# Three one-bank score tiles and three transposed groups in the second attention, where scores have up to 512 columns

## The chip, the core and the metric

The kernel runs on one core of a Trainium2 chip. The metric is the device time of one execution in microseconds: the median of three runs before the change is 2951.13 us (2950.57 to 2956.34). A profiled execution, taken by the hardware profiler, gives the trace that is read below.

The core's engines work side by side, each on its own queue of instructions in a fixed order: TensorE (PE; its weight loads are listed apart as PEld), VectorE (DVE), ScalarE (ACT), GpSimd (POOL) and SyncE (SP), which issues the transfers. TensorE writes its results into PSUM, which this kernel uses as eight banks of 128 x 512 numbers of 4 bytes.

## The reference

One block of a transformer, 1024 positions, width 1024, float32: a gated feed-forward layer, a token mixer, a second feed-forward layer, each after an RMS norm and added to the stream. The mixer has two attentions. The first is a differential attention: 8 heads, each the difference of two softmaxes. The second (`nsa`) has 16 heads in 2 groups and three branches whose outputs are added with gates. One branch works on compressed keys and is done earlier in the kernel. The other two are what the change touches:

```python
s = jnp.where(mask[:, :, :, None], s, NEG_INF)          # selected blocks: at 1024 positions and
p = jax.nn.softmax(s.reshape(sh[:4] + (-1,)), axis=-1)  # 16 blocks of 64, all earlier keys
...
mask = (kpos[None, :] >= 0) & (kpos[None, :] <= qpos[:, None]) & (kpos[None, :] > qpos[:, None] - WIN)
p = jax.nn.softmax(s, axis=-1)                          # window of 512 keys
...
o = g[..., 0:1] * o_cmp + g[..., 1:2] * o_slc + g[..., 2:3] * o_win
```

Since 16 blocks are selected out of 16, the selected branch is causal attention over all earlier keys.

## The kernel before

The kernel runs its stages in this order: first feed-forward layer; the projections of the mixer with the compressed branch (`prelim`); the first attention (`da_phase`); the second (`ns_phase`); the output projections (`proj`); the second feed-forward layer. In the trace the second attention's scores and products lie between about 1478 and 2110 us.

In `ns_phase` the outer loops run over the two groups, then over pairs of heads `pr`, then over the two halves `H` of the positions, then over the two heads `par` of the pair, then over two blocks `m` of 256 queries. For one head and one `m`:

- `ns_scores` takes the two blocks of 128 queries `i = 2m` and `2m+1`. For each it makes two score tiles with `scores`: one of the selected branch, `w = 128 (i+1)` columns, 128 to 1024; one of the window branch, `ww`, at most 640. So in the half `H = 0` (`i` from 0 to 3) no tile has more than 512 columns, and in `H = 1` (`i` from 4 to 7) every tile has at least 640. One pair of heads and one `H` make 16 tiles.
- `scores` writes a tile `S` in PSUM with two matmuls for each piece of columns (L871; over 512 columns in two pieces, one a bank). VectorE adds the mask and takes the row minimum of the negated scores in one instruction (L878, with a short second one that reads the accumulator out). ScalarE takes the exponential into a tile of probabilities in SBUF, `Ps` or `Pw`, and sums the row (L880, again with a short second instruction). Then `S` is free. VectorE inverts the sums (L1034, L1035) and GpSimd scales the probabilities (L1037).
- `ns_pv` multiplies the probabilities by the values. `tr_split` transposes up to four 128 x 128 blocks into a bank `tr` (L926), ScalarE copies it to `th` and VectorE makes the rest `tl` (L89 and L85), each in SBUF; then the matmuls with the values add into the output bank `o` (L1083 with `th`, L1084 with `tl`). The compressed branch opens `o` (L1049), and `ns_fold` empties it (L1092, L1093).

The scores of a block are written in the program ahead of the products of the block before it (`pend`), so that TensorE has products to do while the other engines work on scores. A filler (`fill`) lays gemms of other stages between them at a lower priority and an even pace; these use the bank `gm` (L52 to L54).

The order of the instructions on each engine is not written by hand. A planner runs the program on a model of the engines, takes at each moment the instruction of the highest priority (mostly: the earliest in the program) that the model holds ready, and fixes that order. On the chip each engine then follows it, and waits where what it needs isn't there.

Buffers come from pools. A pool has a number of buffers, and a new tile waits until the last user of its buffer is done. All pools are opened with `reuse_waits="tile"`: a tile in a pool that lies where a closed pool lay waits for the last users of its own bytes (in PSUM, of its own bank) and for nothing else. In both attentions the banks are: two score tiles of two banks each (`sp`), two transposed groups (`tr`), one output bank (`ops`), one for the filler (`gm`). A score tile takes two banks whatever its width. The probabilities have five buffers of each kind (`B_NP`), the `th` and `tl` three (`B_NT`).

Of the kernel before, what the change touches and what calls it, by code (L numbers as in the profile page):

```python
# [7 lines left out]
F32 = mybir.dt.float32  # L8
# [10 lines left out]
P = 128  # L19
T = 1024  # L20
TB = 512
# [840 lines left out]
        nc.sync.dma_start(out=K.s_pc[u * 2 + pr][tb], in_=pp.bitcast(F32))  # L862


def scores(K, passes, w, mask, nm, pt, l):
    nc = K.nc
    S = K.sp.tile([P, T], F32, tag="S", name="S")
    pieces = [(0, 0, w)] if w <= TB else [(0, 0, w // 2), (TB, w // 2, w // 2)]
    for o, c, n in pieces:
        for i, (q, k, k0) in enumerate(passes):  # L870
            K.last = nc.tensor.matmul(S[:, o:o + n], lhsT=q, rhs=k[:, k0 + c:k0 + c + n], start=i == 0, stop=i == 1)  # L871
    if w <= TB:
        sv, mv, pv = S[:, 0:w], mask, pt[:, 0:w]
    else:
        sv = S.rearrange("p (b c) -> p b c", b=2)[:, :, 0:w // 2]
        mv = mask.rearrange("p (b c) -> p b c", b=2)
        pv = pt[:, 0:w].rearrange("p (b c) -> p b c", b=2)
    nc.vector.tensor_tensor_reduce(out=sv, in0=sv, in1=mv, scale=-0.125, scalar=BIG, op0=ALU.add, op1=ALU.min,  # L878
                                   accum_out=nm)
    return nc.scalar.activation(out=pv, in_=sv, func=AF.Exp, scale=-1.0, bias=nm, accum_out=l)  # L880
# [97 lines left out]
def da_load(K, h):  # L978
    drain([da_load_parts(K, h)])
# [317 lines left out]
B_NPC = 2  # L1297
LOW_DA = 20
LOW_NS = 100
TR_DA = 2  # L1300
PACE_DA = 16
PACE_NS = 140

# [1 line left out]
def da_phase(K, cg):  # L1305
    nc = K.nc
    with ExitStack() as ctx:
        K.kp, K.vp, K.qp = open_pool(K, ctx, "dk", B_DK), open_pool(K, ctx, "dv", B_DV), open_pool(K, ctx, "dq", B_DQ)
        K.nk, K.vv = {}, {}
        for n, f in enumerate(da_units(K, 0)[:2] + da_units(K, 1)):  # L1310
            if n == 2:
                early = da_load_parts(K, 0)
            if n >= 2:
                next(early)
            if n == 5:
                q0 = da_queries(K, 0, 0)
            drain([f()])
        cg.close()
        K.low = LOW_DA
        log_exp(K)  # L1320
        K.pp, K.sm, K.tp, K.op = (open_pool(K, ctx, "dp", B_DP), open_pool(K, ctx, "dsm", 6), open_pool(K, ctx, "dt", B_DT),
                                  open_pool(K, ctx, "do", 1))
        K.sp = open_pool(K, ctx, "sp1", 2, True)
        K.tr = open_pool(K, ctx, "tr1", TR_DA, True)
        K.ops = open_pool(K, ctx, "o1", 1, True)
        K.gm = open_pool(K, ctx, "gm1", 3 - TR_DA, True)
        pend = K.fin = None

        def finish(h, m, res):
            if m % 2 == 0:  # L1330
                K.o = K.ops.tile([P, TB], F32, tag="o", name="o")
            if K.fin:
                da_finish2(K, *K.fin)
                K.fin = None
            da_pv(K, h, m, res, K.o)
            if m % 2 == 1:
                K.fin = da_finish(K, h, m // 2, K.o)

        ng = NG_DA // 2
        W = K.A["win"]  # L1340
        units = []
        for p in (2, 3):
            cs = [[C_QDA + 2 * p, C_QDA + 2 * p + 1], [C_KDA + 2 * p, C_KDA + 2 * p + 1], [C_VDA + 2 * p], [C_VDA + 2 * p + 1]]
            units += [(f, [W[c] for c in ws]) for f, ws in zip(da_units(K, p), cs)]
        units += [(f, [W[C_GATE + c]]) for c, f in enumerate(gate_units(K, range(16)))]
        units += [(lambda d=d: pda_unit(K, d), [K.A["wda"][d]]) for d in range(KD)]
        fill = K.filler = Filler(K, units)
        for p in range(4):
            fill.pace(4 * (p + 1) if p < 2 else 8 + ng * (p - 1), PACE_DA)
            for h in (2 * p, 2 * p + 1):  # L1350
                if h:
                    da_load(K, h)
                for m in range(4):
                    qt = q0 if h + m == 0 else da_queries(K, h, m)
                    if h == 4:
                        ns_load_key(K, m)
                    res = da_scores(K, h, m, qt, fill.step)
                    if pend:
                        finish(*pend)
                    pend = (h, m, res)  # L1360
            fill.end()
        finish(*pend)
        da_finish2(K, *K.fin)


def ns_phase(K):
    nc = K.nc
    K.low = LOW_NS
    with ExitStack() as ctx:
# [2 lines left out]
        K.qp, K.kp, K.pcp = open_pool(K, ctx, "nq", 2), open_pool(K, ctx, "nk", 1), open_pool(K, ctx, "npc", B_NPC)  # L1372
        K.pp, K.sm, K.tp, K.op = (open_pool(K, ctx, "np", B_NP), open_pool(K, ctx, "nsm", 6), open_pool(K, ctx, "nt", B_NT),
                                  open_pool(K, ctx, "no", B_NO))
        K.sp = open_pool(K, ctx, "sp2", 2, True)
        K.tr = open_pool(K, ctx, "tr2", 2, True)
        K.ops = open_pool(K, ctx, "o2", 1, True)
        K.gm = open_pool(K, ctx, "gm2", 1, True)
        fill = K.filler
        fill.pace(8 + 16 + KD, PACE_NS)  # L1380
        ns_load_values(K)
# [30 lines left out]
        fill.end()  # L1412
        if pend:
            finish(*pend)


def proj(K, open_x, after):
# [54 lines left out]
def body(tc, A, out):  # L1472
    nc = tc.nc
    K = Ctx()
    K.tc, K.nc, K.A = tc, nc, A
    K.low, K.vv, K.gate, K.fill, K.seen = 0, {}, None, None, {}
    K.h, K.acc, K.R = [None] * 2, [None] * 2, [None] * 2
    with ExitStack() as ctx:
        const = open_pool(K, ctx, "const", 1)
# [172 lines left out]
```

## Time and profile before

| | |
|---|---|
| median of the runs | 2951.13 us (2950.57 to 2956.34) |
| profiled execution | 2957.75 us, span of its instructions 2955.7 us |
| TensorE busy, share of the span | 2830.8 us, 96% |
| TensorE weight loads | 2129.2 us, 72% |
| VectorE | 2002.1 us, 68% |
| ScalarE | 1366.1 us, 46% |
| GpSimd | 788.7 us, 27% |
| mean granted TensorE clock | 0.986 |

How to read it: times are microseconds unless marked ns. A group of instructions is named by its line in the kernel, its engine and what it writes and reads; behind its busy time stands the engine's idle time just before its instructions, and what ended it. A matmul's end is modelled and matmuls overlap in the array, so a busy TensorE can still have slack. A view of stretches gives, for each part of the time, its length and each engine's busy time in it.

### The profile page before, as it was taken

The page shows a single profiled execution, that of the slowest core. Times are in us where ns is not written, and L with a number is a line of the kernel's source. Part 1 is how long each engine was busy: PE and PEld are TensorE (multiplying, and loading weights), DVE is VectorE, ACT ScalarE, POOL GpSimd, SP SyncE. Part 2 cuts the span into 40 slices and gives each one's busy share as a digit, 9 for nine tenths or more (in the row PEclk, how much of TensorE's full clock was granted, in tenths as well). Part 3 has the DMA queues.
Part 4 walks back from the last instruction along what each step waited for, and adds up shares of the span by engine and source line. Part 5 has one row for each costly group of instructions (what it writes and reads, how often), then busy time and mean ns, then how long its engine had stood idle before and what let it go on. Part 6 is the DMA issues. An engine that isn't in the chain of part 4 may idle for free. (4 is left out here: it accounts for less than half of the span.)

```text
span 2955.7 us, 40158 instructions
## 1 busy us (share of the span) xinstructions
PE 2830.8 (96%) x14276; PEld 2129.2 (72%) x14276; DVE 2002.1 (68%) x3347; ACT 1366.1 (46%) x2347; POOL 788.7 (27%) x701
## 2 busy tenths in 40 slices
PE   8999999999999899989899999999999999999998
PEld 6644447888888678778788888888778854444886
DVE  7866856666687467667677777776343877675666
ACT  7543424442332245445466666666332653342443
POOL 3133321000144123322233323332242413333001
PEclk9999999999999999999999999999999999999999
DMA  4355548655456544444332234222742246454854
GB/s 161 129 194 180 182 161 287 214 172 170 146 200 240 173 161 168 170 165 164 122 115 79 86 119 155 79 84 76 281 158 100 89 147 230 149 185 158 297 182 146
DMA packets 212711, 478.20 MB, mean 162 GB/s; under 512 B 20896, under 2 KB 39584, under 8 KB 212512
## 3 DMA queue, kind: packets, MB, share of 16 engines
q1 hardware_dynamic: 212512, 475.65, 47.1%
q8 instruction: 112, 1.84, 0.3%
q14 instruction: 87, 0.71, 0.1%
HBM read 313.56 MB, written 162.00 MB: 161 GB/s over the span
## 5 line engine op out<-in xcount | busy, mean ns | idle before, releaser
L405 PEld LDWEIGHTS <-w 128*128 128x128 f16 x3024 | 297.1, 99 | 381.1 <-issue 30.4
L52 PE MATMUL gm<-hi,whi 128*128 128x512 f32 x880 | 351.5, 399 | 4.0 <-ACT whi L89 1.6
L54 PE MATMUL gm<-hi,wlo 128*128 128x512 f32 x880 | 348.3, 397 | 1.1 <-DVE wlo L85 1.1
L53 PE MATMUL gm<-lo,whi 128*128 128x512 f32 x880 | 348.0, 395 | 0.0
L405 PE MATMUL Y<-tf,w 128*128 128x512 f16 x1296 | 296.7, 383 | 19.1 <-DVE u L443 15.6
L871 PE MATMUL S<-kt,qt 128*128 128x320 f32 (+5 forms) x1152 | 274.6, 352 | 37.5 <-ACT Pt L880 12.0
L85 DVE TENSOR_TENSOR tl<-tr,th 128x512 fp32r<-128x512 f32 (+2 forms) x384 | 236.3, 619 | 89.0 <-ACT th L89 85.5
L89 ACT ACTIVATE th<-tr 128x512 fp32r<-128x512 f32 (+2 forms) x384 | 203.7, 542 | 200.4 <-PE tr L926 195.6
L85 DVE TENSOR_TENSOR wlo<-st,whi 128x1024 fp32r<-128x1024 f32 x154 | 197.6, 1300 | 113.5 <-ACT whi L89 112.2
L878 DVE CUSTOM_DVE_ANT_0 S<-S,slab 128x896 f32<-128x896 f32 (+7 forms) x320 | 224.7, 709 | 65.8 <-PE S L871 61.3
L53 PE MATMUL acc<-wlo,whi 128*128 128x512 f32 (+1 forms) x628 | 244.1, 389 | 1.0 <-DVE wlo L85 1.0
L89 ACT ACTIVATE whi<-st 128x1024 fp32r<-128x1024 f32 x154 | 160.7, 1057 | 178.2 <-PE acc L54 111.6
L54 PE MATMUL acc<-whi,wlo 128*128 128x512 f32 (+1 forms) x628 | 242.8, 389 | 0.0
L52 PE MATMUL acc<-whi 128*128 128x512 f32 (+1 forms) x628 | 240.4, 387 | 0.0
L871 PEld LDWEIGHTS S<-kt,qt 128*128 128x128 f32 x1152 | 183.4, 190 | 61.5 <-ACT Pt L880 13.8
L1037 POOL TENSOR_SCALAR Ps<-Ps,l 128x384 f32<-128x384 f32 (+7 forms) x128 | 100.7, 787 | 428.6 <-DVE l L1035 214.4
L405 PE MATMUL X<-h,w 128*128 128x512 f16 x864 | 195.3, 379 | 0.5 <-ACT s L415 0.5
L52 PEld LDWEIGHTS gm<-hi,whi 128*128 128x128 f32 x880 | 168.3, 191 | 37.2 <-ACT whi L89 2.2
L54 PEld LDWEIGHTS gm<-hi,wlo 128*128 128x128 f32 x880 | 167.8, 191 | 37.3 <-DVE wlo L85 1.8
L53 PEld LDWEIGHTS gm<-lo,whi 128*128 128x128 f32 x880 | 168.1, 191 | 30.9
L85 DVE TENSOR_TENSOR wlo<-wst,whi 128x1024 fp32r<-128x1024 f32 x103 | 135.8, 1320 | 45.4 <-ACT whi L89 36.1
L1083 PE MATMUL o<-th,vt 128*128 128x256 f32 (+1 forms) x608 | 165.0, 288 | 1.6 <-ACT th L89 1.5
(320 smaller groups left out, 6128.7 us busy)
## 6 DMA issues: line engine op xcount, KB each, us to landing
wst<-in_win_dram SPq DMA_DIRECT2D x55, 512.0 KB
sw<-w2s SPq DMA_DIRECT2D x44, 512.0 KB
st<-sw SPq DMA_DIRECT2D x88, 256.0 KB
st<-saT SPq DMA_DIRECT2D x88, 256.0 KB
a<-in_f1w_dram SPq DMA_DIRECT2D x36, 512.0 KB
a<-in_f2w_dram SPq DMA_DIRECT2D x36, 512.0 KB
st<-saB SPq DMA_DIRECT2D x66, 256.0 KB
qt<-sq SPq DMA_DIRECT2D x128, 128.0 KB
```

The costliest lines, as they stand in the source:

```text
L52: first = nc.tensor.matmul(out, lhsT=w[0][:, wk], rhs=x[0], start=start, stop=False, skip_group_check=skip)
L53: nc.tensor.matmul(out, lhsT=w[0][:, wk], rhs=x[1], start=False, stop=False, skip_group_check=skip)
L54: nc.tensor.matmul(out, lhsT=w[1][:, wk], rhs=x[0], start=False, stop=stop, skip_group_check=skip)
L85: return nc.vector.tensor_tensor(out=lo, in0=src, in1=hi.bitcast(F32), op=ALU.subtract)
L89: nc.scalar.activation(out=hi, in_=src, func=AF.Copy)
L405: K.mark = nc.tensor.matmul(o, lhsT=w[:, a, m * h + k], rhs=x[k][:, b], start=start and k == 0 and i == 0, stop=k == h - 1 and i == 2, ski ...
L871: K.last = nc.tensor.matmul(S[:, o:o + n], lhsT=q, rhs=k[:, k0 + c:k0 + c + n], start=i == 0, stop=i == 1)
L878: nc.vector.tensor_tensor_reduce(out=sv, in0=sv, in1=mv, scale=-0.125, scalar=BIG, op0=ALU.add, op1=ALU.min, accum_out=nm)
L1037: nc.gpsimd.tensor_scalar(out=p[:, 0:n], in0=p[:, 0:n], scalar1=l[:, c:c + 1], scalar2=1.0, op0=ALU.mult, op1=ALU.mult)
L1083: nc.tensor.matmul(dst, lhsT=v, rhs=hi[:, b * P:(b + n) * P], start=False, stop=False, skip_group_check=True)
```

## The change

Score tiles are now taken by `score_tile`, which knows two layouts of the same six banks. The wide one is that of before: two tiles of two banks, two transposed groups. The narrow one has three tiles of one bank and three transposed groups. In the second attention (`K.narrow = True`) a tile of up to 512 columns asks for the narrow layout, any other for the wide one; where the layout differs from the present one, the two pools are closed and opened anew. As every `H = 0` is narrow and every `H = 1` wide, the layout changes with every `H`: 16 layouts in the phase. The products that come after a change in the program take their `tr` from the new layout. In the first attention `K.narrow` is off, and the layout is the wide one throughout. So that the six banks lie together, `gm` and `ops` are now opened first, from the other end of PSUM.

```diff
+def score_tile(K, w):
+    n = 1 if K.narrow and w <= TB else 2
+    if K.s_banks != n:
+        close_scores(K)
+        K.s_banks = n
+        K.sp = open_pool(K, K.s_ctx, "sp", (3, 2)[n - 1], True)
+        K.tr = open_pool(K, K.s_ctx, "tr", (3, 2)[n - 1], True)
+    return K.sp.tile([P, n * TB], F32, tag="S", name="S")
+
+
+def close_scores(K):
+    K.s_ctx.close()
+    K.s_ctx, K.s_banks = ExitStack(), 0
+
+
 def scores(K, passes, w, mask, nm, pt, l):
     nc = K.nc
-    S = K.sp.tile([P, T], F32, tag="S", name="S")
+    S = score_tile(K, w)
...
-TR_DA = 2
...
-        K.sp = open_pool(K, ctx, "sp1", 2, True)
-        K.tr = open_pool(K, ctx, "tr1", TR_DA, True)
-        K.ops = open_pool(K, ctx, "o1", 1, True)
-        K.gm = open_pool(K, ctx, "gm1", 3 - TR_DA, True)
+        K.narrow = False
+        K.gm = open_pool(K, ctx, "gm1", 1, True, side="right")
+        K.ops = open_pool(K, ctx, "o1", 1, True, side="right")
...
         da_finish2(K, *K.fin)
+        close_scores(K)
...
-        K.sp = open_pool(K, ctx, "sp2", 2, True)
-        K.tr = open_pool(K, ctx, "tr2", 2, True)
-        K.ops = open_pool(K, ctx, "o2", 1, True)
-        K.gm = open_pool(K, ctx, "gm2", 1, True)
+        K.narrow = True
+        K.gm = open_pool(K, ctx, "gm2", 1, True, side="right")
+        K.ops = open_pool(K, ctx, "o2", 1, True, side="right")
...
             finish(*pend)
+        close_scores(K)
...
+    K.s_ctx, K.s_banks = ExitStack(), 0
```

`open_pool` and the `ExitStack` are those of before: closing the stack closes the two pools, in the reverse order of opening.

## The prediction

> **What bounds the kernel now.** I read the page first, then the stretches of the second attention, the waits in it, and the groups of TensorE's instructions by shape.
>
> ```profile
> span 2955.7 us, 40158 instructions
> ...
> PE 2830.8 (96%) x14276; PEld 2129.2 (72%) x14276; DVE 2002.1 (68%) x3347; ACT 1366.1 (46%) x2347; POOL 788.7 (27%) x701
> ...
> PE   8999999999999899989899999999999999999998
> ```
>
> TensorE is busy nearly everywhere, so time can only be won where it stands still, and only there. The second attention runs from about 1478 us (slice 20 of 40) to about 2110 us. I cut it at every sixteenth score tile on VectorE: one such stretch holds the scores of one pair of heads for one half H of the queries. H=0 has scores of at most 512 columns (light), H=1 has 640 to 1024 on one branch and 640 on the other (heavy). The view of stretches gives, for each, start and end, length, then busy time of PE, PEld, DVE, ACT and POOL, the granted clock and the DMA share. The rows alternate light, heavy:
>
> ```profile
> 1477.70:1500.40 22.70, 20.22 (x100) 15.75 (x100) 16.48 (x55) 14.11 (x41) 10.49 (x17) 1.00 0.55 202
> 1500.40:1539.50 39.10, 38.50 (x254) 34.92 (x252) 30.57 (x72) 26.53 (x55) 13.39 (x16) 1.00 0.22 79
> 1539.50:1578.20 38.70, 35.99 (x233) 31.48 (x233) 26.87 (x77) 21.61 (x57) 9.90 (x16) 1.00 0.21 78
> 1578.20:1616.10 37.90, 37.47 (x246) 34.13 (x244) 30.69 (x70) 26.08 (x54) 13.80 (x16) 1.00 0.27 90
> 1616.10:1654.80 38.70, 36.13 (x237) 31.84 (x237) 27.11 (x77) 21.57 (x57) 9.04 (x16) 1.00 0.22 71
> 1692.30:1730.40 38.10, 36.70 (x241) 32.43 (x240) 26.63 (x77) 22.63 (x60) 9.62 (x16) 1.00 0.23 76
> 1767.50:1808.90 41.40, 38.74 (x234) 34.15 (x233) 26.44 (x77) 21.68 (x57) 10.07 (x16) 0.92 0.77 224
> 1846.90:1885.00 38.10, 35.74 (x233) 31.39 (x233) 25.71 (x75) 22.78 (x59) 9.08 (x16) 1.00 0.21 70
> 1922.90:1960.90 38.00, 36.11 (x235) 31.89 (x235) 25.40 (x74) 22.79 (x59) 9.10 (x16) 1.00 0.23 77
> 1998.10:2037.90 39.80, 36.77 (x236) 32.07 (x236) 25.47 (x75) 22.76 (x59) 9.94 (x16) 1.00 0.26 89
> ```
>
> Length less PE busy is TensorE's idle time. The eight light stretches have 2.48, 2.71, 2.57, 1.40, 2.66, 2.36, 1.89 and 3.03 us: 19.1 us together. The two heavy ones shown have 0.60 and 0.43. No other engine is full: VectorE, the next, is busy 26.87 of 38.70 us in a light stretch. So the change works where the phase's standstill is, and 19.1 us (0.65% of the time) is all that stands open to view there.
>
> What ends that standstill: the waits of the whole phase (us in total, times, longest), then TensorE's groups by shape (busy, mean ns, idle just before and its releaser).
>
> ```profile
> ACT Pw L880 <- PE tr L926: 41.3, 27, 5.8
> ...
> PE S L871 <- ACT Ps L880: 7.1, 14, 1.0
> ...
> PE o L1084 <- DVE tl L85: 5.5, 19, 0.5
> PE o L1049 <- DVE y L1093: 5.2, 7, 1.1
> ...
> PE S L871 <- ACT Pw L880: 3.3, 8, 0.9
> ...
> PE o L1083 <- ACT th L89: 1.5, 6, 0.5
> ```
>
> ```profile
> L871 PE MATMUL S<-kt,qt 128*128 128x320 f32 x320 | 65.2, 326 | 1.3 <-ACT Ps L880 0.7 <-ACT Pw L880 0.4
> ...
> L871 PE MATMUL S<-kt,qt 128*128 128x512 f32 x128 | 40.0, 417 | 0.5 <-ACT Ps L880 0.2
> L871 PE MATMUL S<-kt,qt 128*128 128x384 f32 x128 | 33.4, 365 | 0.9
> ...
> L871 PE MATMUL S<-kt,qt 128*128 128x256 f32 x64 | 15.4, 331 | 3.2 <-ACT Pw L880 2.1 <-ACT Ps L880 1.0
> L871 PE MATMUL S<-kt,qt 128*128 128x128 f32 x60 | 12.5, 290 | 6.1 <-ACT Ps L880 5.2 <-ACT Pw L880 0.9
> ```
>
> A score matmul that waits for an exponential of another head waits for a score tile to come free. These waits are 7.1 + 3.3 = 10.4 us, in 22 places, none over 1.0. By shape they lie in the narrow tiles: 6.1 + 3.2 + 0.9 + 0.5 = 10.7 us stand before tiles of 128 to 512 columns (the 512 and 384 rows hold halves of wide tiles too, and little).
>
> **The change part by part.** No compute instruction is added or removed; its matmuls, evictions and DMAs are those of before. In the first attention the flag is off and the pools come to the same banks, so I price it at nothing. That leaves three parts, all in the second.
>
> *Third score tile.* It takes the place of the wait for the exponential two tiles back; the wait becomes one for three tiles back. A light stretch makes 16 tiles in 38 us, 2.4 us apart, and the longest wait is 1.0 us; so with the order kept, one tile more of slack ends all of them: -10.7 us. But the order is planned anew: the planner puts a score matmul as early as its model says a tile is free, and with three tiles it can come just as close to the release again. Then nothing is won: 0. I take two thirds, -7.1 us, because waits of half a microsecond (10.4 / 22 = 0.47) are short against the 2.4 us spacing; both ends stay for the range.
>
> *Third transposed group.* A group is filled by TensorE, copied on ScalarE, subtracted on VectorE, then multiplied. TensorE waits for the copy or the difference 5.5 + 1.5 = 7.0 us in the phase. One light stretch has this share:
>
> ```profile
> L1083 PE MATMUL o<-th,vt 128*128 128x256 f32 x30 | 9.0, 310 | 0.2 <-ACT th L89 0.2
> L1084 PE MATMUL o<-tl,vt 128*128 128x256 f32 x30 | 8.5, 303 | 0.6 <-DVE tl L85 0.6
> ```
>
> That is 0.8 us, times seven full light stretches 5.6 us. The split copies in SBUF have three buffers already; what is late is the difference, not a free bank, and a third bank only lets the transposes start sooner. I take a third, -2.0 us (bounds 0 and -5.6).
>
> *Sixteen changes of layout.* A new tile waits only for the last users of its own banks, so there is no drain, and nothing is issued for it. From wide to narrow, the first two narrow tiles lie on the two banks of the older wide tile: no worse than before. From narrow to wide it is worse: sixteen narrow tiles end on bank 0, so the first wide tile (banks 0 and 1) waits for the very last narrow exponential, where before it waited for the last but one. Behind it in TensorE's queue stand the transposes and products of the previous query block and the filler's gemms, and VectorE and ScalarE wait for those. The chain it would wait out is that of a 512-column tile:
>
> ```profile
> L878 DVE DVE_READ_ACCUMULATOR2_ANT nm<- 128x1 f32 x256 | 35.7, 139 | 0.1
> ...
> L878 DVE CUSTOM_DVE_ANT_0 S<-S,slab 128x512 f32<-128x512 f32 x32 | 22.1, 692 | 2.2 <-PE S L871 1.5
> ```
>
> ```profile
> L880 ACT ACTIVATION_READ_ACCUMULATOR Ps<-S,nm 128x1 f32 x128 | 25.3, 198 | 0.0
> ...
> L880 ACT ACTIVATE Ps<-S,nm 128x512 f32<-128x512 f32 x16 | 11.0, 687 | 6.8 <-PE tr L926 3.4 <-DVE tl L85 1.5 <-DVE nm L878 1.3
> ```
>
> 0.69 + 0.14 + 0.69 + 0.20 = 1.72 us, at eight places 13.8 us if nothing covers it. The cover is the products and the filler, which the planner can put ahead of the wide scores; they keep TensorE at 38.50 of 39.10 us in a heavy stretch. I take 0.3 us each, +2.4 us (bounds 0 and 13.8). If the cover fails, the filler is what comes late, and after it the projection.
>
> The wait for the single output bank (L1049, 5.2 us) is not touched. The sum: -7.1 - 2.0 + 2.4 = -6.7 us. The profiled execution took 2957.75 us (span 2955.7, and 2.05 around it), which becomes 2951.0. It stands 6.6 us over the median of the runs, 2951.13; taken from the median, the forecast is 2944.4, so **2944 us**.
>
> **A rule that speaks against it.** The granted clock is 1.00 in nine of the ten stretches shown, and the standstills come in pieces of at most 1.1 us. The Trainium skill, "TensorE: Matmul & The Clock Gate", section on HAM oscillation, reports that once a kernel kept TensorE warm, "Adding PSUM double-buffering gave no further gain". This trace agrees that TensorE is warm; by that rule the sum would be 0 and the time about 2951, as in the first rival.
>
> **The rivals.**
>
> *The probability buffers limit, not the score banks (no change).* ScalarE's exponential waits 41.3 us for transposes to give a buffer of Pw back, four times what TensorE waits for score tiles. While it does, any number of score tiles fill up and the last one waits again. Against it: the waits of TensorE name the narrow tiles, and there probabilities are small work. The third tile then only brings the subtraction ahead: the 10.7 us stay, the groups give -2.0 and the switches take 0 to 2.4: 2949 to 2951, say 2950.
>
> *The switch costs what it bounds (slower).* This is the wait at the first wide tile, uncovered. It decides from 9.1 / 8 = 1.1 us at each change, where the gain is gone; at the full 1.72 us, and with the planner putting the narrow tiles back to their releases, it is -2.0 + 13.8 = +11.8: 2963; with the half of it left uncovered and no gain, 2951 + 6.9 = 2958. For it speaks that the scores run a block ahead of the products, and that this head start is what is cut at each change; against it, the cover above. I put 2960.
>
> *A larger gain.* All the idle time of the light stretches goes: 2951 - 19 = 2932. For it: busy PE hides part of the standstill, since ends are modelled. Weight loads fill 31.48 of 38.70 us in a light stretch and 34.92 of 39.10 in a heavy one, 81% against 89%. Against it: the output bank's 5.2 us cannot go. The Trainium skill, "Perfetto Trace Analysis", section Identifying the Most-Contended Engine, holds weight-load busy time to be the better measure of headroom; by its measure a light stretch has 8% of 38 us, some 3 us, to win, 21 us over seven, an estimate close to this rival's 19.
>
> **How the numbers follow.** The forecast's case has 0.40, no change 0.25, slower 0.25, the larger gain 0.10. What this kernel's runs can tell from no change is 0.2%, 5.9 us: below 2945.2 is faster, above 2957.0 slower. The forecast case is itself uncertain by the planner's share: 0.34 of its 0.40 lies below 2945.2, 0.06 above. So faster is 0.34 + 0.10 = 0.44, within 0.2% is 0.25 + 0.06 = 0.31, slower is 0.25. The range reaches from the larger gain's 2932 to 2962, just short of the full price of the switches; I leave a tenth out on either side. The forecast case alone spans 2936 to 2948 (all of the first two parts' bounds with the chosen switch: -10.7 - 5.6 + 2.4 = -13.9 is 2937; a third of the first, -3.6 alone, is 2947.5).
>
> **What would show it.** Right: the waits of narrow score matmuls for an exponential fall from 10.7 to about 4 us, light stretches shorten by about 1 us each, heavy ones keep their length within 0.3 us. The probability rival: those waits stay near 10 us and ScalarE still waits some 41 us for transposes. The slow rival: the 320-column row's idle time (now 1.3 us) rises to 7 us or more, at eight places. The larger gain: light stretches at 36 us. Wrong altogether: a time that moves by more than 6 us with these rows unchanged, or a change outside 1478 to 2110 us; that would be the planner's new order, which I did not price.

## The result and the profile after

The kernel after takes 2930.38 us (median of six runs, 2926.57 to 2935.09) against 2953.65 us for the kernel before (median of six, 2950.57 to 2956.34): ratio 0.9923, 95% interval 0.9910 to 0.9936. That is 23.3 us or 0.8% faster. It is faster as forecast, but by three and a half times as much as the 6.7 us of the sum, and it lies 1.6 us below the low end of the range.

The profiled execution after took 2929.13 us, 28.6 us less than the 2957.75 us of the profiled execution before. 5 of these 28.6 us are scatter: the one stood 4 us over its kernel's median, the other 1 us under it. The head of its page and the TensorE row of the forty slices:

```profile
span 2927.3 us, 40127 instructions
...
PE 2813.9 (96%) x14276; PEld 2122.4 (73%) x14276; DVE 2003.0 (68%) x3347; ACT 1364.6 (47%) x2347; POOL 789.2 (27%) x701
...
PE   8999999999999899989989999999999999999998
```

Little on this page but the length tells the two kernels apart. TensorE is 96% busy in both, although its busy time fell by 17 us with the same 14276 matmuls. Part of that may be the clock's: the run with the narrow layout off (below) has the order of instructions of before on every engine, a mean granted clock of 0.990 instead of 0.986, and 2825.3 us of busy time, 11 us more than after. So the busy time itself holds something that the change took away.

Where it lies is shown by the view of stretches, cut as before at every sixteenth score tile on VectorE (start and end, length, busy time of PE, PEld, DVE, ACT, POOL, the granted clock, DMA share, GB/s); the rows alternate light and heavy, and start with a light one:

```profile
1474.00:1507.90 33.90, 24.93 (x130) 21.49 (x131) 19.98 (x62) 17.73 (x48) 12.25 (x19) 0.85 0.41 151
1507.90:1545.80 37.90, 37.52 (x246) 34.03 (x245) 30.08 (x71) 25.69 (x53) 12.49 (x15) 1.00 0.23 82
1545.80:1580.50 34.70, 33.93 (x233) 30.86 (x232) 26.51 (x78) 21.76 (x58) 10.99 (x18) 1.00 0.26 86
1580.50:1618.30 37.80, 37.35 (x247) 34.00 (x246) 30.04 (x72) 25.75 (x53) 12.10 (x15) 1.00 0.26 90
1618.30:1653.10 34.80, 34.64 (x236) 31.48 (x236) 26.73 (x77) 21.94 (x58) 10.14 (x18) 1.00 0.28 87
1690.40:1726.20 35.80, 34.87 (x234) 31.31 (x234) 25.89 (x78) 21.55 (x58) 10.10 (x18) 1.00 0.26 85
1911.50:1947.60 36.10, 34.94 (x236) 31.55 (x236) 26.19 (x76) 22.87 (x60) 10.49 (x18) 1.00 0.26 90
```

The light stretches after the first fell from about 38 us (38.70, 38.70, 38.10 at these places before) to about 35 (34.70, 34.80, 35.80). All seven together went from 272.8 to 247.6 us, so 25.2 us. Some 3 of these seem to be the clock's: one of the seven before, 41.4 us long, has a granted clock of 0.92, and with the narrow layout off the same place takes 38.8 us at 1.00 and the seven 269.9, so that the fall is 22.3 us. The six heavy ones between them went from 225.6 to 226.6. Only the first light stretch grew, from 22.7 to 33.9 us, at a granted clock of 0.85. A wait of 7.2 us on VectorE, which the profile puts down to the store of the first attention's output (`syd`), now lies inside it; before, one of 7.9 us on ScalarE for the same store lay just ahead of it, at 1465 us, in the first attention. So the second attention as a whole fell by less than its light stretches, from 632.8 to 615.4 us in the view of stretches.

TensorE's groups of score matmuls by shape, and the opening matmul of `o`, in the second attention after (busy, mean ns, then idle time just before and its releaser; L886 is the old L871, L1064 the old L1049):

```profile
L886 PE MATMUL S<-kt,qt 128*128 128x320 f32 x320 | 60.9, 316 | 0.3 <-ACT Pw L895 0.2
...
L886 PE MATMUL S<-kt,qt 128*128 128x512 f32 x128 | 39.4, 415 | 1.4 <-ACT Pw L895 1.2
L886 PE MATMUL S<-kt,qt 128*128 128x384 f32 x128 | 32.8, 357 | 0.4 <-ACT Pw L895 0.4
L1064 PE MATMUL o<-pc,vc 128*128 128x512 f32 x64 | 21.3, 415 | 0.6 <-DVE y L1108 0.6
...
L886 PE MATMUL S<-kt,qt 128*128 128x256 f32 x62 | 13.9, 309 | 1.0 <-ACT Ps L895 1.0
L886 PE MATMUL S<-kt,qt 128*128 128x128 f32 x60 | 11.4, 284 | 0.2 <-ACT Pw L895 0.2
```

The waits ahead of narrow tiles fell from 10.7 to 3.0 us (1.4 + 0.4 + 1.0 + 0.2), which is what the forecast said would show it right. But two more things moved. The wait for the output bank, said to be untouched, fell from 5.2 to 0.6 us. And the visible idle time of the seven light stretches fell from 16.6 to 5.3 us, 11.3 us, while they became 22 to 25 us shorter. About half of the gain was never counted as idle.

**Where the rest was.** A matmul's end is modelled, and idle time is counted from that end. Two matmuls that follow each other start much closer than one of them is said to last. A place in the light stretch before, TensorE alone (start, duration, instruction, idle before it in brackets):

```profile
1920.35 0.28 PE L1084 MATMUL o<-tl,vt 128*128 128x256 f32 x1
...
1920.90 0.38 PE L1083 MATMUL o<-th,vt 128*128 128x256 f32 x1
1921.63 0.39 PE L1084 MATMUL o<-tl,vt 128*128 128x256 f32 x1 [0.34 <-DVE tl L85]
1921.85 0.28 PE L1083 MATMUL o<-th,vt 128*128 128x256 f32 x1
1921.97 0.28 PE L1084 MATMUL o<-tl,vt 128*128 128x256 f32 x1
```

Undisturbed, the next product starts 0.12 us after the one before (1921.85 to 1921.97). At the wait it starts 0.73 us after (1920.90 to 1921.63). So 0.61 us is lost and 0.34 shown, and a wait of under some 0.25 us (0.38 that the matmul is said to last, less 0.12) is not shown at all. I summed these excesses: the gap from one matmul's start to the next one's, less the median gap of its line and shape in the second attention, wherever it is over 1.4 times that median. Over the seven light and six heavy stretches this *standstill by starts* is 58.4 us before and 36.6 after; the 13 stretches themselves went from 498.3 to 474.2. The difference in standstill (21.8) is nearly the difference in length (24.1). In the light ones alone it is 40.0 before and 21.7 after, against 16.6 and 5.3 us of visible idle. With the narrow layout off, where no low clock lies in these stretches, the 13 take 495.7 us with 58.1 of standstill, so length and standstill both fall by 21.5 us to the kernel after. The amount hangs on the rule: with the line and shape of the later matmul instead, the light stretches have 45.0 us before and 30.9 after.

### The profile page after: what moved, and what is told of

It is laid out like the page before. It is cut to its first block, busy times and chain, and to the rows that moved or that the text cites. A ratio compares the mean times of both kernels' runs of the same rounds, so it can differ in the third digit from the quotient of the medians.

```text
span 2927.3 us, 40127 instructions
## 1 busy us (share of the span) xinstructions
PE 2813.9 (96%) x14276; PEld 2122.4 (73%) x14276; DVE 2003.0 (68%) x3347; ACT 1364.6 (47%) x2347; POOL 789.2 (27%) x701
## 5 line engine op out<-in xcount | busy, mean ns | idle before, releaser
L886 PE MATMUL S<-kt,qt 128*128 128x320 f32 (+5 forms) x1152 | 264.0, 348 | 26.3 <-ACT Pt L895 9.6
L886 PEld LDWEIGHTS S<-kt,qt 128*128 128x128 f32 x1152 | 184.5, 190 | 43.6 <-ACT Pt L895 11.4
L1099 PE MATMUL o<-tl,vt 128*128 128x256 f32 (+1 forms) x608 | 159.3, 294 | 15.3 <-DVE tl L85 15.1
```

The lines of the kernel that those rows point to most:

```text
L1099: nc.tensor.matmul(dst, lhsT=v, rhs=lo[:, b * P:(b + n) * P], start=False, stop=last, skip_group_check=True)
```

## The experiments

All were compared with the kernel before, which had medians between 2952.6 and 2953.7 us in these comparisons. Edits are to the kernel after unless said otherwise. First, whether the new structure costs or gives something with the old numbers of buffers.

**No narrow layout at all.**

```diff
-        K.narrow = True
+        K.narrow = False
```

> The changed kernel with the narrow layout switched off in the second attention as well: two wide score tiles and two transposed groups throughout, only the order in which the pools are opened is that of the change. All theories: the plan of the kernel before, ratio 1.000 within 0.002 (about 2953 us). If it is faster by more than that, opening the pools in another order is itself a cause.

2952.55 us, ratio 1.0000 (0.9991 to 1.0009). The pools opened from the other end of PSUM change nothing that can be measured, and in the traces every engine has the order of instructions of before.

**Narrow layout with two score tiles and two groups.** Score tiles of one bank, all sixteen changes of layout, but no buffer more than before.

```diff
-        K.sp = open_pool(K, K.s_ctx, "sp", (3, 2)[n - 1], True)
-        K.tr = open_pool(K, K.s_ctx, "tr", (3, 2)[n - 1], True)
+        K.sp = open_pool(K, K.s_ctx, "sp", (2, 2)[n - 1], True)
+        K.tr = open_pool(K, K.s_ctx, "tr", (2, 2)[n - 1], True)
```

> Narrow layout of two one-bank score tiles and two transposed groups (two banks idle): the sixteen changes of layout without a buffer more. Buffer theory: no gain, only the price of the changes, 0 to +14 us, so 2953 to 2967 us. Planner theory (the gain is the luck of a new order): it moves by 10 us or more in some direction without a buffer more, to 2943 or below if the luck is like that of the change.

2951.66 us, 1.0000 (0.9989 to 1.0012). The sixteen changes cost nothing that can be measured in the whole time, and this new order of the planner's is not faster by itself. By stages there is more to see, in single executions: the second attention takes 634.0 us (first exponential to last fold) against 629.9 with the narrow layout off, and the output projections behind it 175.4 against 180.8. So the changes may cost some 4 us in their own stage, with as much won back behind it.

**One buffer more of one kind.** Three score tiles and two groups; then two score tiles and three groups.

```diff
-        K.tr = open_pool(K, K.s_ctx, "tr", (3, 2)[n - 1], True)
+        K.tr = open_pool(K, K.s_ctx, "tr", (2, 2)[n - 1], True)
```

> Narrow layout with three score tiles and two transposed groups (one bank idle). Theory S (the third score tile carries the gain, 7.1 of 9.1 us in the forecast's sum): at least three quarters of the 23 us, 2930 to 2936 us. Theory G (the third group carries it): at most 6 us, 2947 us or more.

2974.76 us, 1.0074 (1.0059 to 1.0089): the third score tile alone makes the kernel 23 us slower than the run with two and two.

```diff
-        K.sp = open_pool(K, K.s_ctx, "sp", (3, 2)[n - 1], True)
+        K.sp = open_pool(K, K.s_ctx, "sp", (2, 2)[n - 1], True)
```

> Narrow layout with two score tiles and three transposed groups (one bank idle). Theory S: a gain of at most 6 us, 2947 us or more. Theory G: at least three quarters of the 23 us, 2930 to 2936 us. If this and the run with three score tiles each bring about half, both parts carry it.

2925.94 us, 0.9910 (0.9896 to 0.9925): the third group alone brings 25.7 us against two and two, the whole gain. In the profiled executions of these two the second attention falls from 634.0 to 608.1 us, and the parts ahead of it and behind it by about 2 us each. The two parts of the change have opposite signs. On top of three groups the third score tile changes 2925.94 into 2930.38; the intervals overlap, so there it is no gain and perhaps a loss of 4 us.

TensorE's own waits from 1545 to 2090 us (us in total, times, longest), for two and two, then for two score tiles and three groups:

```profile
PE o L1099 <- DVE tl L85: 5.8, 21, 0.5
PE o L1064 <- DVE y L1108: 3.5, 7, 0.5
PE S L886 <- ACT Pw L895: 3.3, 9, 0.6
PE S L886 <- ACT Ps L895: 2.2, 6, 0.4
PE o L1098 <- ACT th L89: 1.2, 4, 0.4
```

```profile
PE o L1099 <- DVE tl L85: 5.3, 17, 0.5
PE o L1064 <- DVE y L1108: 2.7, 4, 0.9
PE S L886 <- ACT Pw L895: 1.4, 6, 0.4
PE o L1098 <- ACT th L89: 0.3, 2, 0.2
PE S L886 <- ACT Ps L895: 0.2, 1, 0.2
```

The sums are 16.0 and 9.9 us: the view of waits shows 6 of the 26 us. The standstill by starts shows 58.1 and 38.0, so 20, beside 23.9 us by which these 13 stretches became shorter (498.9 to 475.0). The third bank even helps the score matmuls (5.5 us of waits to 1.6), with no score tile more. The third score tile alone leaves them at 4.5 us, while the waits ahead of the products (`th` and `tl`) more than double:

```profile
PE o L1099 <- DVE tl L85: 11.8, 39, 0.6
PE o L1064 <- DVE y L1108: 7.3, 7, 1.1
PE o L1098 <- ACT th L89: 4.4, 16, 0.4
PE S L886 <- ACT Ps L895: 2.5, 7, 0.6
PE S L886 <- ACT Pw L895: 2.0, 5, 0.7
```

In the seven light stretches the third group takes the standstill by starts from 40.3 to 21.9 us. Sorted by the matmul that starts late, it falls from 17.6 to 7.1 us ahead of scores, from 17.0 to 10.6 ahead of products and from 5.4 to 3.5 ahead of the opening of `o`. Ahead of transposes it is 0.4 and 0.6. So TensorE hardly stands where the group's bank itself is needed; the planned order seems to put other work there, and the time is lost further on.

**The dose of groups.** Two score tiles, and four groups, or one:

```diff
-        K.sp = open_pool(K, K.s_ctx, "sp", (3, 2)[n - 1], True)
-        K.tr = open_pool(K, K.s_ctx, "tr", (3, 2)[n - 1], True)
+        K.sp = open_pool(K, K.s_ctx, "sp", (2, 2)[n - 1], True)
+        K.tr = open_pool(K, K.s_ctx, "tr", (4, 2)[n - 1], True)   # the other run: (1, 2)
```

> Two narrow score tiles and four transposed groups, six banks in use. Theory T (two groups cap the products: a group holds its bank for 2.33 us in a light stretch, so two give one group in 1.17 us, and TensorE needs about 0.92 us for one; three give one in 0.9 us): the cap is gone with three, a fourth brings within 6 us of the run with two and three, 2920 to 2932 us. If the slack of more groups goes on paying: below 2918 us.

> Two narrow score tiles and one transposed group: one step down on the scale 1, 2, 3, 4 of which 2, 3 and 4 gave 2952, 2926 and 2924 us. Theory T (turnover of the group's bank): with one bank a group follows the other after 2.33 us or more; a light stretch has about 21 groups, so at least 21 x 2.33 = 49 us instead of 39, eight times +10: 3030 us or more. If the bank is not what holds the products and the third group gained only by another order, one group costs about as much as the third brought: 2975 to 2990 us.

Four groups: 2924.04 us, 0.9894 (0.9879 to 0.9909). One: 3100.75 us, 1.0500 (1.0479 to 1.0521). With one, two, three and four groups the time is 3100.75, 2951.66, 2925.94 and 2924.04 us. The first bank more is worth 149 us, the second 26, the third 2, which is within the scatter.

A reason can be read from a group's hold of its bank. In the light stretches before, the mean from the first transpose to the end of the subtraction is 2.33 us: 0.55 to fill it, 0.34 until the copy starts, 0.54 for the copy, 0.28, and 0.61 for the subtraction. Two banks pass one group in 2.33 / 2 = 1.17 us. TensorE's own work on a group is four transposes 0.11 us apart and four products 0.12 us apart, 0.92 us. Where nothing else stands between groups, TensorE outruns two banks by a quarter of a microsecond a group; three banks pass one in 2.60 / 3 = 0.87 us (2.60 is the hold after), which is below 0.92, and a fourth has nothing left to win. This is an estimate from means. The traces bear it out where three or more groups of a light stretch follow each other with no score matmul or filler between: their first transposes start 1.14 us apart before and 1.24 with three score tiles and two groups, but 0.84 after, 0.87 with two score tiles and three groups, and 0.61 with four. Before there are only 15 such spacings, which make some 4 of the 18 us of standstill. How the bank brings the rest, through the planner's new order, is not shown.

With one group, a light and a heavy stretch (columns as above):

```profile
1554.90:1617.80 62.90, 51.40 (x251) 41.24 (x250) 28.27 (x79) 23.63 (x60) 10.97 (x18) 0.78 0.19 63
1617.80:1654.70 36.90, 36.31 (x234) 32.49 (x234) 29.05 (x69) 24.68 (x51) 12.12 (x15) 1.00 0.20 71
```

The heavy one, which has two groups there too, is as it was. The light one takes 62.9 us, and the granted clock falls to 0.78 in it. So up to 14 of these 62.9 us (22%) are the low clock's, and up to 77 of the 417.9 us that the seven light stretches take: the 149 us are not the wait for the bank alone.

**Three groups in both attentions.** Two narrow score tiles as above, and in the first attention too:

```diff
-        K.narrow = False
+        K.narrow = True
```

> Two narrow score tiles and three transposed groups in both attentions (the first has eight columns widths too, 128 to 1024, half of its tiles narrow, and three matmuls per block of products instead of two). Theory T carried over: the first attention has 80 groups where the second has 304, half of the products in it light, so a quarter of the gain or less comes on top: 2918 to 2926 us. If the first attention is held by other waits (its exponential and its sums of two), no more: 2924 to 2932 us, or slower.

2959.06 us, 1.0019 (1.0009 to 1.0030). The second attention keeps its gain, but the last transposes of the first end at 1510 us instead of 1476. There TensorE stands for transfers (26.5 us for `vt`, against 3.0 before, by its view of waits), and the whole gain is lost there. Why these transfers are waited for longer stays open.

**Why is the third score tile a loss?** The first theory was that it shares a bank with others: the second wide tile lies on a bank of the narrow transposed groups. With the two groups always in banks 4 and 5 this is undone:

```diff
-        K.tr = open_pool(K, K.s_ctx, "tr", (3, 2)[n - 1], True)
+        K.tr = open_pool(K, K.s_ctx, "tr", (2, 2)[n - 1], True, side="right")
```

> Three narrow score tiles and two transposed groups again, which lost 22 us, but the two groups stay on the two banks they have in the wide layout too (the idle bank lies between), so a group no longer shares a bank with the second wide score tile. Theory W (the loss comes at the end of the light stretch, where the first wide scores wait for the last light products to leave that bank, and TensorE has nothing else to do): most of the 22 us comes back, 2948 to 2960 us. Theory Q (the third tile brings score work ahead of the evictions of the groups on ScalarE and VectorE all along): it stays at 2968 us or more.

2970.99 us, 1.0053 (1.0037 to 1.0069). Some 4 of the 23 us come back, no more than scatter allows, where this theory asked for most of them. And with four score tiles and two groups:

```diff
-        K.sp = open_pool(K, K.s_ctx, "sp", (3, 2)[n - 1], True)
-        K.tr = open_pool(K, K.s_ctx, "tr", (3, 2)[n - 1], True)
+        K.sp = open_pool(K, K.s_ctx, "sp", (4, 2)[n - 1], True)
+        K.tr = open_pool(K, K.s_ctx, "tr", (2, 2)[n - 1], True)
```

> Four narrow score tiles and two transposed groups, six banks in use. Theory Q: score work runs still further ahead, slower than with three: above 2975 us. Theory W: the groups lie on the banks of before, apart from the wide tiles, so near the kernel before, 2948 to 2960 us.

2967.05 us, 1.0042 (1.0028 to 1.0056): a loss again, and no larger than that of three. That contradicts both theories as written.

The second theory was that more score tiles let the planner put scores too early, being earlier in the program. So `ns_scores` called its score tiles through a function that gives the narrow ones a lower priority, with three and two, in the kernel before, and with two and four:

```diff
+def late_scores(K, *a):
+    if a[1] > TB:
+        return scores(K, *a)
+    with K.tc.high_priority(offset=-60):
+        return scores(K, *a)
```

> Three narrow score tiles and two groups (2975 us, 22 slower), with the narrow scores' instructions 60 places lower in the planner's priorities, so that they yield to the products of the block before. Order theory (the third tile hurts because it lets scores run ahead of products): most of the 22 us comes back, 2950 to 2960 us. If the tile hurts by itself: 2968 us or more.

> The kernel before with the same lower priority for scores of up to 512 columns. With two tiles the scores can't run as far ahead, so order theory: within 10 us of before, 2943 to 2963 us. If it gains as much as the third group (27 us), the order of scores and products was the whole matter and the banks only a way to change it.

> Two narrow score tiles and four groups (2924 us) with the same lower priority. Order theory: products no longer interrupted, 2914 to 2922 us; if scores come too late to feed the next block: 2930 us or more.

2974.27 us (1.0074, 1.0059 to 1.0089), 2953.21 (0.9998, 0.9988 to 1.0007) and 2921.24 (0.9895, 0.9881 to 0.9910). None differs from its partner beyond the scatter. In the traces the kernel before with late scores has the order of before on every engine, and TensorE's order with the other two differs from that of their partners in 8 and in 17 of 14276 places. So this edit moved next to nothing, and neither shows the theory nor refutes it.

What the trace of three and two shows stands at the end of a light stretch, ahead of the first wide scores. TensorE, then VectorE, then ScalarE:

```profile
1900.15 0.39 PE L1098 MATMUL o<-th,vt 128*128 128x256 f32 x1 [0.39 <-ACT th L89]
1900.75 0.39 PE L1099 MATMUL o<-tl,vt 128*128 128x256 f32 x1 [0.21 <-DVE tl L85]
...
1902.70 1.09 PE L1064 MATMUL o<-pc,vc 128*128 128x512 f32 x2 [1.05 <-DVE y L1108]
1903.59 0.41 PE L1098 MATMUL o<-th,vt 128*128 128x256 f32 x1
1903.80 0.41 PE L1099 MATMUL o<-tl,vt 128*128 128x256 f32 x1
...
1905.19 1.91 PE L886 MATMUL S<-kt,qt 128*128 128x320 f32 x8
```

```profile
1906.54 0.83 DVE L893 CUSTOM_DVE_ANT_0 S<-S,slab 128x640 f32<-128x640 f32 x1 [3.43 <-PE S L886]
```

```profile
1907.53 0.80 ACT L895 ACTIVATE Ps<-S,nm 128x640 f32<-128x640 f32 x1 [5.08 <-DVE nm L893]
```

The scores' head start has run dry. TensorE has only transposes and products left and waits for each group's copy and difference, then for the output bank. Then the products follow at 0.21 us instead of 0.12 (1903.59 to 1903.80), half the pace, at a granted clock of 0.50 from 1902.9 to 1906.3 us, and only after them come the wide scores, for which VectorE had waited 3.4 and ScalarE 5.1 us. The kernel after at the same place, with the same sharing of banks but three groups, ScalarE:

```profile
1873.95 0.80 ACT L895 ACTIVATE Ps<-S,nm 128x640 f32<-128x640 f32 x1 [1.61 <-DVE nm L893]
```

At the seven places of this kind ScalarE stands 3.5 to 5.3 us ahead of the first wide exponential with three and two, 1.6 after and 1.7 with two and two. From the last narrow score matmul to the first wide one it takes 10.5 us with three and two (mean of the seven), 6.1 after and 7.7 with two and two. The 2.8 us more at seven places come near the loss. But where the groups lie apart, in banks 4 and 5, these are only 5.5 us, and the loss is spread over the heavy stretches instead (standstill by starts 30 us against 16). So the dry spot is where the loss falls with shared banks, and not all of its cause.

The clock has a part in this profile too. Two light stretches with three and two (columns as above):

```profile
1705.20:1748.80 43.60, 39.43 (x240) 33.81 (x240) 26.06 (x77) 22.00 (x58) 10.60 (x18) 0.97 0.27 86
1864.50:1906.50 42.00, 38.81 (x240) 33.52 (x239) 25.71 (x75) 22.90 (x60) 11.56 (x18) 0.96 0.23 79
```

Spells at half clock make up to 6.8 us in the 13 stretches, which are 16.8 us longer than with two and two. With the groups apart there is no such spell in them, and they are 7.5 us longer still, so the clock is not the whole loss either. What the light stretches have more of standstill by starts than before (59.8 against 40.0 us) lies all ahead of products (36.8 against 16.7).

**Cover by the filler.** If it is the lack of other work between the groups, more filler in the light stretches should cover it. The filler's pace was doubled in light stretches and set to nought in heavy ones, or set to 1.5 and 0.5:

```diff
-    def step(self):
+    def step(self, share=1.0):
...
-        self.due += self.rate
+        self.due += self.rate * share
...
-                            res = ns_scores(K, hd, m, qt, g, fill.step)
+                            res = ns_scores(K, hd, m, qt, g, lambda: fill.step(2.0 if H == 0 else 0.0))
```

In the kernel before, with 2 and 0 and with 1.5 and 0.5:

> The kernel before, two wide score tiles and two groups, with the filler's gemms all laid into the light stretches: twice the pace at H=0, none at H=1. Nothing else changes. Cover theory (TensorE stands still in light stretches because between a group's transposes and its products it has too little other work, and three groups replace that cover): about half of the 40 us of standstill in the light stretches goes, the heavy ones lose little, 2930 to 2942 us. Pure turnover theory: filler cannot free a bank, so the light stretches get longer by the gemms they take (15 k-steps of 0.7 us, 10 us each) and the heavy ones shorter by as much: 2948 to 2958 us.

> The kernel before with the filler's pace by 1.5 where H is 0 and by 0.5 where H is 1: the partner of the run with three score tiles and this pace. Doubled and nought cost 4 us; this is expected within 3 us of the kernel before by either theory, 2950 to 2956.

2957.28 us (1.0018, 1.0009 to 1.0028) and 2942.68 us (0.9965, 0.9954 to 0.9976). The first is outside what the cover theory expected. With 2 and 0 the standstill by starts falls in the light stretches from 40.0 to 31.1 us and rises in the heavy ones from 18.4 to 37.1: the cover is needed in both. That 1.5 and 0.5 gain 10 us was not expected. In the profiled pair the second attention is 4 us shorter and the output projections behind it 7; the cause is open.

With two score tiles and four groups:

> Two narrow score tiles and four groups (2924 us) with all of the filler in the light stretches. If cover still lacks in them (some 20 us of standstill are left): 2908 to 2918 us. If four groups have replaced the cover, the heavy stretches now lack the filler: 2924 us or slower.

> As the run before, with three quarters of the filler in the light stretches and a quarter in the heavy ones. Cover theory: the best of all, 2906 to 2916 us. Otherwise within 6 us of 2924 us.

2952.62 us (1.0000, 0.9991 to 1.0009) and 2926.19 us (0.9909, 0.9894 to 0.9923), so 29 us lost and nothing gained against even filler. A fourth bank leaves the light stretches little to cover. With three score tiles and two groups:

> Three narrow score tiles, two transposed groups, and the filler's pace doubled where H is 0 and nought where H is 1. In the light stretches of the kernel with three score tiles and two groups, 67 of 140 groups follow the one before with no score matmul and no filler gemm between them, 1.21 us apart; with two score tiles and two groups it is 68 of 150, 0.73 us apart, and the runs of three or more such groups hold 38 groups against 25. Theory of bare products (the third tile lets scores run ahead, and what is left at the end of a light block is a run of groups with nothing between, at the pace of two banks): twice the filler in the light stretches covers those runs, the loss of 22 us against the kernel before with the same filler (2957.3) shrinks to under 8 us: 2957 to 2965, and the spacing of uncovered groups in light stretches falls below 0.9 us. Rival (the third tile's loss does not hang on what stands between the groups): the 22 us stay: 2975 to 2983.

> Three narrow score tiles, two transposed groups, and the filler's pace by 1.5 where H is 0 and by 0.5 where H is 1. Theory of bare products: half of the cover of the doubled pace, the distance to the kernel before with the same filler falls from 22 to 8 to 15 us. Rival: it stays at 20 to 24 us.

2989.94 us (1.0127, 1.0109 to 1.0145) and 2960.09 us (1.0028, 1.0018 to 1.0037): 32.7 and 17.4 us over the kernel before with the same filler, where 22 was the loss with even filler. The first contradicts the theory of bare groups as I wrote it, and the second lies between the two expectations. By starts, the excess of three and two over the kernel before in the light stretches does fall with more filler there: 59.8 - 40.0 = 19.8 us, then 48.2 - 31.8 = 16.4, then 43.7 - 31.1 = 12.6. That points to lack of cover as a part of it, and doesn't show it: the light stretches themselves are longer than those of the kernel before with the same filler by 19, 23 and 30 us. And in the bare heavy stretches of 2 and 0 a new wait comes up, wide scores waiting for exponentials:

```profile
PE S L886 <- ACT Ps L895: 19.4, 32, 1.1
```

What makes a third or fourth score tile cost 13 to 23 us with two groups stays open.

**The best version** measured has two score tiles and three or four groups: 2925.94 and 2924.04 us, with late scores 2921.24. The three can't be told apart. Against the kernel after, three groups can't either; the interval of four ends (0.9909) where that of the kernel after begins (0.9910), so four with two score tiles is probably the better kernel, by some 6 us.

## Why the prediction was wrong where it was

**The third transposed group: -2.0 forecast, -25.7 measured.** This is the step that failed. Its bounds, 0 and -5.6, came from 0.8 us of visible waits in a light stretch times seven. That sum holds only what sticks out beyond a modelled matmul end. By starts, TensorE stood still 40.0 us in these stretches, and the third bank took some 18 of them (40.0 to 21.7 in the change, 40.3 to 21.9 from two and two to two and three). The sentence "what is late is the difference, not a free bank" failed with it: a late difference holds its bank, so the next transposes come late and the next difference after them (1.14 us apart where groups follow each other bare, 0.84 after). In this ring of copy and difference, a wait for its last link was also a lack of buffers; 2.33 us of hold over two banks against 0.92 us of work could have been worked out from the trace before. That two banks are too few is shown by the runs with one to four; the way from the bank to most of the 18 us is not.

**The third score tile: -7.1 forecast, +23 measured with two groups, nothing or +4 with three.** The sign was wrong. Its observable came out right (narrow score waits 10.7 to 3.0 us), and yet it was no evidence: the score waits fall from 5.5 to 1.6 us with the third group alone, and only to 4.5 with the third score tile alone. The waits that were named after score tiles went with the groups' bank. So that the kernel became faster at all, as forecast, is luck: the term that carried the forecast was a loss.

**The sixteen changes of layout: +2.4 forecast, 0 measured** (two and two, within 3.5 us either way; perhaps 4 in their own stage and as much won behind it). The cover that was named holds: the idle time ahead of 320-column tiles, said to rise to 7 us if it failed, is 0.3 us. The first attention at nothing was right (2952.55 us with the narrow layout off). The heavy stretches were to keep their length within 0.3 us: their sum nearly did (225.6 to 226.6 us), single ones moved by up to 1.1. The output bank "not touched" was wrong, 5.2 to 0.6 us. Why is open: it is 2.7 with two score tiles and three groups, and 0.7 with three and two apart, where the products do stand.

**The rivals.** The probability buffers as the limit fell by its own signs, though no run changed these buffers: the waits of narrow scores went, and ScalarE's waits for transposes to give back `Pw` halved, from 41.3 to 19.5 us:

```profile
ACT Pw L895 <- PE tr L941: 19.5, 19, 2.2
```

The switch as a slow case fell; what it described, a head start cut at the change to wide, appeared only where three score tiles met two groups. The larger gain, 2932 us, was the nearest. It had the right grounds (busy PE hides standstill; weight loads fill 81% of a light stretch) and the right sign of them (light stretches at 36 us; they are at 35.4). It got a chance of 0.10 because "the output bank's 5.2 us cannot go". The weight loads answer: 31.48 of 38.70 us before, 30.86 of 34.70 after, so 81% became 89% (87 to 90% in the four full light stretches shown after), about the share that the heavy stretches had all along. The Trainium skill, "Perfetto Trace Analysis", section Identifying the Most-Contended Engine, was the better guide here: the 21 us worked out with it stand beside the 22 to 25 measured in these seven stretches. It told the size, and not which buffer would bring it.

**The rule that spoke against it.** "Adding PSUM double-buffering gave no further gain" (the Trainium skill, "TensorE: Matmul & The Clock Gate", section on HAM oscillation) is said there of one matmul kernel, and does not carry over to this ring: 2951.66 us with two groups became 2925.94 with three, and the granted clock was 1.00 in nine of the ten stretches shown before and in six of seven after. A warm TensorE is not a TensorE without standstill.

**What moved outside the second attention.** The stage of the output projections, just behind it (columns as above), before and after:

```profile
2110.80:2293.40 182.60, 178.63 (x764) 143.74 (x763) 62.91 (x72) 57.35 (x73) 68.26 (x45) 0.99 0.46 162
```

```profile
2089.90:2265.30 175.40, 175.40 (x764) 143.16 (x763) 64.09 (x72) 57.78 (x73) 68.04 (x45) 1.00 0.49 169
```

7.2 us of the 28.6 of the profiled pair went here, with no change to this stage. Before, 4.0 of them are idle time of TensorE (182.60 less 178.63 us, after none), mostly for the rest of a split (`wlo`) that VectorE makes:

```profile
PE pj L54 <- DVE wlo L85: 2.0, 2, 1.2
PE po L54 <- DVE wlo L85: 1.5, 1, 1.5
PE po L52 <- ACT whi L89: 0.4, 1, 0.4
```

A spell at half clock before (0.99 in its row) makes up to 1.7 more. It is not the banks: the run with two and two also has 175.4 us here and is no faster than the kernel before, and the kernel before with uneven filler has 175.3. Why the split comes late only there stays open. The forecast had named a change outside 1478 to 2110 us as a sign of the planner's new order, which it did not price; this is one. The second attention also begins 4 us earlier after, but in three executions of the order of before it begins at 1472.9, 1477.7 and 1481.3 us, so that is scatter. I count neither as the buffers' doing.

## What to carry to other kernels

Work out a ring of buffers from its hold time: the time one buffer is held, divided by the number of buffers, against the work of the engine that it feeds. Where the first is larger, one more buffer can pay, whichever wait the trace names; here it paid 26 us. To see a standstill of TensorE, compare the starts of its matmuls with the spacing of an undisturbed row of them; idle time between modelled ends shows only part of it. When a change gives two kinds of buffers more room at once, run each kind alone: here one brought 26 us and the other cost 23 alone.

## What the runs showed of the hardware that I had not expected

**Matmuls start closer than they last.** 0.12 us apart with 256 columns, each said to last 0.28 us or more; a stop of 0.61 us showed as 0.34. **Where TensorE stood still much, its clock was low.** With one group the granted clock was 0.78 in a light stretch and 1.00 in the next heavy one, and 0.961 over the span against 0.989 after. With three and two, products started 0.21 us apart instead of 0.12 just behind a stop of 1.05 us, at a granted clock of 0.50. So a stop can be paid for twice. That the stops bring the clock down is read from the order in time and not tested: in the kernel before, one light stretch is at 0.92 in one execution and at 1.00 in another of the same order.
